# The output projection of a hybrid attention block: from eight row-and-column products to a 2x2 block product in seven multiplications

## The chip, the cores and the metric

One core of one Trainium2 chip runs the whole program. The metric is device microseconds (us) of one execution. The engines are TensorE (PE in the profile; its weight loads are PEld), VectorE (DVE), ScalarE (ACT), GpSimd (POOL) and SyncE (SP, which only issues transfers). Each engine works through its own queue in order and waits on semaphores.

## The reference, cut to what matters

A block of 512 tokens and width 1024: a gated linear attention and a latent attention run side by side, their outputs are merged by two gates, and the merged rows are projected and added to the residual. A feed-forward layer follows.

```
merged = sigmoid(z_ma) * y_gla + sigmoid(z_mb) * y_mla      # 512 x 1024
h = h + merged @ w_out                                      # 1024 x 1024 weights
m = rmsnorm(h, g_mlp)
h = h + square(relu(m @ w_ff1)) @ w_ff2
return rmsnorm(h, g_final)
```

All of it is float32. The kernel multiplies on TensorE in fp32r: each operand is split into a high and a low part (`split`, line 92: ScalarE rounds the high part, another engine subtracts it), and one product is three matmuls, high by high, high by low and low by high (`mm3`, line 87).

## The kernel before, in words

The work is laid out with features on partitions (transposed) up to the merge. `g2`, `y1` and `merged` hold one 128x512 tile for each of the eight latent heads: 128 features by 512 tokens.

**Attention** (lines 1134 to 1148). A loop over n from 0 to 37 takes one quarter of a head at each step: scores of quarter n (`att_scores`, line 903), the flip of the probabilities of quarter n-3 by TensorE transposes (`att_flip`, 921), and the values of half a head at n-6 (`att_values`, 932). Beside them `up_units` (849) projects the queries, keys and values of the next pair of heads; GpSimd subtracts the low parts of its weights. After the second half of a head VectorE multiplies the values by the gate (944) and GpSimd adds the other branch (945). A planner (the tile framework's scheduler) fixes each engine's order when the program is built, by trace order as priority and by the buffers that are free; `in_program_order` (110) overrules it for the engines that it names, from a mark on.

**Output projection** (lines 1149 to 1244). After the loop the eight merged tiles are scaled by 0.5 and split (1151). `rows_product` (1163) then makes, for each half c of the 1024 output columns, four accumulators of 128 tokens by 512 columns, each over eight feature tiles k: 2 x 4 x 8 = 64 products, 192 matmuls of 128x512. The weights come in pieces of 256 rows (`weights`, 218). For c = 1 the last two pieces are kept back so that the rows are finished one after the other: a row's sum is added to the residual `h` by VectorE (`add_rows`, 1210), squared by ScalarE (`square_half`, 171), its reciprocal root made by VectorE and GpSimd (`row_rstd`, 178), scaled by VectorE (`normed`, 1226) and turned by eight TensorE transposes (`flipped`, 1237; `Flipped.rows`, 191), and after every second row the turned tiles are read out of PSUM and split by ScalarE and VectorE (`Flipped.evacuate`, 201).

**Feed-forward** (lines 1416 to 1472). Two projections, f00 and f01, are begun early (1416, 1417 to 1424): their first half runs before the last two rows are turned. The second matrix product of each quarter already is a 2x2 block product in seven multiplications (`prep` 1275, `pair_units` 1321, `block_product` 1352): sums of blocks of the left and right side are multiplied, and the results are added to the rows.

**Buffers.** Tiles of one tag share a fixed number of buffers: 29 of 2 KB a partition (`u2`), 26 of 4 KB (`u4`), 3 staging tiles for weights (`stage`, 209), and four each for the high and the low parts of weights (`halves`, 213). A new tile waits until the last reader of the oldest buffer is done.

```
    def halves(nk, nw, name):
        wh = tl([P, nk, nw], F32R, "wh", 4, f"{name}h")
        wl = tl([P, nk, nw], F32R, "wl", 4, f"{name}l")
```

Of the kernel before, what the change touches and what calls it, by code (L numbers as in the profile page):

```python
# [18 lines left out]
P = 128  # L19
# [37 lines left out]
def tile_block(ctx: ExitStack, tc: tile.TileContext, t, out: bass.AP):  # L57
# [113 lines left out]
    def square_half(rows, c, parts, junk):  # L171
        nc.scalar.activation(
            junk[:, c * S : (c + 1) * S], rows[:, c * S : (c + 1) * S], AF.Square, accum_out=parts[:, c : c + 1]
        )
        if c == 0:
            nc.gpsimd.tensor_scalar(parts[:, 2:3], parts[:, 0:1], 1.0 / D, EPS, op0=ALU.mult, op1=ALU.add)
# [207 lines left out]
    nc.vector.tensor_scalar(gla_gain, gvec[:, V_GLA : V_GLA + 8], 0.5, None, op0=ALU.mult)  # L384
# [461 lines left out]
    merged = [None] * MH  # L846
    heads = {}

    def up_units(pr):
# [37 lines left out]
        for j in range(2):  # L887
# [7 lines left out]
            split(hl[:, 0].rearrange("p a b -> p (a b)"), hl[:, 1].rearrange("p a b -> p (a b)"), acc)  # L895
# [36 lines left out]
    def att_values(head, half):  # L932
        if half == 0:
            avs[head] = ps("mm", f"av{head}")
        acc = avs[head]
        hi, lo = pTs.pop((head, half))
        _, _, vs, c = heads[head]
        for k in range(NT):
            vt = vs[k // 2]
            mm3(acc[:, half * 256 : (half + 1) * 256], vt[:, 0, k % 2, c], vt[:, 1, k % 2, c],  # L940
                hi[:, k, :], lo[:, k, :], k == 0, k == NT - 1)
        if half == 1:
            y = g2[head]
            nc.vector.scalar_tensor_tensor(y, y, 1.0, acc, op0=ALU.add, op1=ALU.mult)  # L944
            nc.gpsimd.tensor_tensor(y, y, y1[head], op=ALU.add)  # L945
            merged[head] = y
# [186 lines left out]
    units = iter(())  # L1133
    for n in range(4 * MH + LAG_C):
# [6 lines left out]
        if 0 <= b < 4 * MH:  # L1141
            flips = traced()
            att_flip(b // 4, b % 4)
            if b == 0:
                gla_turn(GH - 1, (flips, traced()))
        c = n - LAG_C
        if c >= 0 and c % 2 == 1:
            att_values(c // 4, (c % 4) // 2)
    for i in range(MH):
        hl = u4(f"mg{i}")  # L1150
        split_scaled(hl[:, 0, :], hl[:, 1, :], merged[i], 0.5)
        merged[i] = hl


    hrow = []
    for i in range(NT):
        r = u4(f"h{i}", F32, (P, D))
        nc.scalar.dma_start(r, t["x"][0, i * P : (i + 1) * P, :])
# [4 lines left out]
    def rows_product(lhs, w, nk, name, first_done, done, flip):  # L1163
        for c in range(2):
            accs = [ps(("mm", "at")[c], f"{name}{c}{i}") for i in range(NT)]

            def piece(i, k2, wh, wl):
                tok = slice(i * P, (i + 1) * P)
                for kk in range(2):
                    k = 2 * k2 + kk  # L1170
                    mm3(accs[i], lhs[k][:, 0, tok], lhs[k][:, 1, tok], wh[:, kk, :], wl[:, kk, :],
                        k == 0, k == nk - 1)

            staggered = 2 if c == 1 else 0
            kept = []
            for k2 in range(nk // 2):
                wh, wl = weights(w[k2 * 2 * P : (k2 + 1) * 2 * P, c * S : (c + 1) * S], f"{name}{c}{k2}")
                if k2 >= nk // 2 - staggered:
                    kept.append((k2, wh, wl))
                    continue  # L1180
                for i in range(NT):
                    piece(i, k2, wh, wl)
            if c == 0:
                for i in range(NT):
                    add_rows(i, c, accs[i])
                    first_done(i)
                continue
            begun = traced()
            ks = [(2 * k2 + kk, wh[:, kk, :], wl[:, kk, :]) for k2, wh, wl in kept for kk in range(2)]

            def part(i, which):
                tok = slice(i * P, (i + 1) * P)
                for k, wh, wl in ks[which]:
                    mm3(accs[i], lhs[k][:, 0, tok], lhs[k][:, 1, tok], wh, wl, k == 0, k == nk - 1)

            def complete(i):
                add_rows(i, c, accs[i])
                done(i)

            for i in range(2):  # L1200
                part(i, slice(0, 4))
                complete(i)
            for i in range(2):
                part(2 + i, slice(0, 2 - i))
                flip(i)
                part(2 + i, slice(2 - i, 4))
                complete(2 + i)
            return begun

    def add_rows(i, c, acc):  # L1210
        hc = hrow[i][:, c * S : (c + 1) * S]
        nc.vector.tensor_tensor(hc, acc, hc, op=ALU.add)  # L1212

    fm = Flipped(gvec[:, V_MLP : V_MLP + 8], "m")
    mT = fm.out
    w1, w2 = t["w_ff1"][0], t["w_ff2"][0]
    ms_rows = {}

    def first_half_square(i):
        hparts[i] = sm(f"hp{i}", 4)  # L1220
        ms_rows[i] = u4(f"ms{i}", F32, (P, D))
        square_half(hrow[i], 0, hparts[i], ms_rows[i])
# [3 lines left out]
    def normed(i):  # L1226
        at = traced()
        m = ms_rows[i]
        square_half(hrow[i], 1, hparts[i], m)
        rs = row_rstd(hparts[i])  # L1230
        for c in range(2):
            nc.vector.tensor_scalar(
                m[:, c * S : (c + 1) * S], hrow[i][:, c * S : (c + 1) * S], rs, None, op0=ALU.mult
            )
# [9 lines left out]
    begun = rows_product(merged, t["w_out"][0], KD, "wo", first_half_square, normed, flipped)  # L1244

    NQ = 4
    FQ = DFF // P // NQ  # L1250
    NP = FQ // 2
    HT = S // 2
    B11, B12, B21, B22 = range(4)
    wq = [[u4(f"w2_{x}{g}", F32, (P, 2, S)) for g in range(NP // 2)] for x in range(4)]

    def load_w2(qd, x):
        for g in range(NP // 2):
            for pp_ in range(2):
                r = (qd * FQ + 2 * (2 * g + pp_) + x // 2) * P
                c = (x % 2) * S  # L1260
                nc.sync.dma_start(wq[x][g][:, pp_, :], w2[r : r + P, c : c + S])

    def add_w2(dst, x, y, op):
        for g in range(NP // 2):
            nc.vector.tensor_tensor(wq[dst][g], wq[x][g], wq[y][g], op=op)  # L1265

    def split_w2(x, name):
        res = []
        for g in range(NP // 2):
            wh, wl = halves(2, S, f"{name}{g}")  # L1270
            split(wh, wl, wq[x][g])
            res.append((wh, wl))
        return res

    def prep(m, qd):

        more = qd + 1 < NQ
        if m == 1:
            return split_w2(B11, f"b1_{qd}")
        if m == 2:  # L1280
            res = split_w2(B21, f"b2_{qd}")
# [3 lines left out]
        if m == 3:  # L1285
            return split_w2(B22, f"b3_{qd}")
        if m == 5:
            add_w2(B11, B12, B11, ALU.subtract)
            return split_w2(B11, f"b5_{qd}")
        if m == 6:  # L1290
            add_w2(B11, B22, B11, ALU.subtract)
            return split_w2(B11, f"b6_{qd}")
        if m == 7:
            add_w2(B12, B22, B12, ALU.subtract)
            res = split_w2(B12, f"b7_{qd}")
# [5 lines left out]
        res = split_w2(B11, f"b4_{qd}")  # L1301
# [19 lines left out]
    def pair_units(qd, p, a22):  # L1321
# [7 lines left out]
        a11, a12, a21, a22_ = px[:, 0:HT], px[:, HT:S], qx[:, 0:HT], qx[:, HT:S]  # L1329
        y, z = u2(f"y{qd}{p}"), u2(f"z{qd}{p}")  # L1330
        s1, s2, s3, s4 = y[:, 0:HT], y[:, HT:S], z[:, 0:HT], z[:, HT:S]
        g1 = u4(f"ga{qd}{p}")
        split(g1[:, 0, :], g1[:, 1, :], px)
        nc.vector.tensor_tensor(s1, a21, a22_, op=ALU.add)
# [166 lines left out]
```

## Time and profile before

| | us |
|---|---|
| median of 3 runs (769.06 to 769.26) | 769.13 |
| the profiled execution, its own time | 769.4 |
| its span, first to last instruction | 767.7 |
| PE busy in the span | 758.5 |
| DVE busy | 571.4 |
| ACT busy | 441.8 |
| POOL busy | 119.1 |

The profiled execution's time is 1.7 us above its span: what lies before the first and behind the last instruction. Shares of busy time are means over stages with different limits, so a change in one stage is read from that stage. A row of a timeline gives the start, the duration, the engine, the line, the operation, the tile written, the tiles read, the shapes and the count; in square brackets stands the engine's idle time before it and what ended it. A row's duration begins when the engine takes the instruction up, so that a wait for a shared port is part of the duration.

### The profile page before, as it was taken

The numbers are of one execution on the slowest core, as the hardware profiler recorded it, in microseconds if no ns is written. First come the engines' busy times: TensorE is split into PE (matmuls) and PEld (weight loads), VectorE is DVE, ScalarE is ACT, GpSimd is POOL, SyncE is SP. The second block draws the span as 40 slices with busy tenths as digits, with TensorE's granted clock in tenths as the row PEclk, the third lists the DMA queues.
The fourth block names the chain that finished last, engine by engine and source line by source line (L and its number), as shares of the span: only waits on it lengthen the run. The fifth ranks groups of instructions, "written<-read, shape, count | busy, mean of one in ns | idle before, by whom it ended". The sixth has DMA issues, their size and how long they took to land.

```text
span 767.7 us, 10149 instructions
## 1 busy us (share of the span) xinstructions
PE 758.5 (99%) x3768; PEld 641.4 (84%) x3768; DVE 571.4 (74%) x850; ACT 441.8 (58%) x749; POOL 119.1 (16%) x190
## 2 busy tenths in 40 slices
PE   9999999999999999999999999999999999999996
PEld 7888788889888889889988988888888888888885
DVE  7789999656767765999944776975887478848695
ACT  7556567465466555888833566434653555346644
POOL 0710005260624105111200100000000000000014
PEclk9999999999999999999999999999999999999998
DMA  9733211221334324221043721353115510550002
GB/s 314 248 111 118 81 28 28 56 77 36 85 80 108 60 53 110 73 66 55 29 165 87 270 83 56 99 181 104 55 55 175 155 30 26 188 168 1 27 1 109
DMA packets 93185, 73.94 MB, mean 96 GB/s; under 512 B 15088, under 2 KB 74480, under 8 KB 93136
## 3 DMA queue, kind: packets, MB, share of 16 engines
q1 hardware_dynamic: 92048, 70.14, 31.0%
q10 hardware_dynamic: 864, 2.38, 0.8%
q0 software_dynamic: 224, 0.79, 0.3%
q8 instruction: 29, 0.48, 0.3%
q14 instruction: 20, 0.16, 0.1%
HBM read 69.62 MB, written 2.10 MB: 93 GB/s over the span
## 4 chain that ended last, share of the span: by engine, by line
PE 96%; DVE 2%; ACT 1%; issue 0%; POOL 0%; POOLq 0%; ACTq 0%
PE f L89 8%; PE f L90 8%; PE f L88 8%; PE gx L88 4%; PE gx L89 4%; PE gx L90 4%; PE first L325 3%; PE za L88 2%; PE za L89 2%; PE wo L89 2%; PE wo L90 2%; PE gz L89 2%; PE za L90 2%; PE gz L88 2%; PE wo L88 2%; PE gz L90 2%
## 5 line engine op out<-in xcount | busy, mean ns | idle before, releaser
L1440 POOL DMA_DIRECT2D gfin<-in_g_final x1 | 0.7, 653 | 282.7 <-PE f L90 282.7
L1265 DVE TENSOR_TENSOR w<-w,w 128x1024 f32<-128x1024 f32 x32 | 38.7, 1221 | 0.4
L913 ACT ACTIVATE e<-s,top 128x512 f32<-128x512 f32 x32 | 21.8, 683 | 4.3 <-DVE top L910 4.3
L473 POOL COPY v3f<-rrf 128x4 f32<-128x4 f32 x4 | 2.8, 708 | 135.9 <-DVE rrf L456 135.9
L1212 DVE TENSOR_TENSOR h<-gx,h 128x512 f32<-128x512 f32 x32 | 21.6, 685 | 1.9 <-PE gx L90 1.8
L94 DVE TENSOR_TENSOR pT<-tp,pT 128x512 fp32r<-128x512 f32 x32 | 21.6, 679 | 0.6 <-ACT pT L93 0.4
L910 DVE TENSOR_REDUCE top<-s 128x1 f32<-128x512 f32 x32 | 21.6, 680 | 0.1
L93 ACT ACTIVATE pT<-tp 128x512 fp32r<-128x512 f32 x32 | 18.9, 592 | 3.4 <-PE tp L927 3.3
L945 POOL TENSOR_TENSOR tb<-tb,za 128x512 f32<-128x512 f32 x8 | 11.2, 1401 | 52.8 <-DVE tb L944 38.4
L927 PE MATMUL tp<-ident,e 128*128 128x128 f32 x128 | 19.2, 272 | 0.0
L88 PE MATMUL av<-pT,v 128*128 128x256 f32 x64 | 19.2, 300 | 0.0
L1318 ACT ACTIVATE fa<-f 128x512 f32<-128x512 f32 x32 | 18.5, 578 | 0.0
L89 PE MATMUL av<-pT,v 128*128 128x256 f32 x64 | 18.4, 288 | 0.0
L927 PEld LDWEIGHTS tp<-ident,e 128*128 128x128 f32 x128 | 15.5, 140 | 3.5 <-PE s L90 0.6
L90 PE MATMUL av<-pT,v 128*128 128x256 f32 x64 | 18.2, 285 | 0.0
L93 ACT ACTIVATE gbh<-y 128x512 fp32r<-128x512 f32 x16 | 10.1, 634 | 14.0 <-DVE y L1335 14.0
L94 DVE TENSOR_TENSOR sc<-sc,sc 128x512 fp32r<-128x512 f32 x16 | 10.9, 690 | 9.5 <-ACT sc L93 9.5
L93 ACT ACTIVATE sc<-sc 128x512 fp32r<-128x512 f32 x16 | 9.3, 596 | 11.5 <-DVE sc L544 11.5
L88 PE MATMUL s<-kbuf,q 96*128 96x512 f32 x32 | 13.9, 434 | 0.6 <-ACT e L913 0.3
L93 ACT ACTIVATE b_20h<-w 128x1024 fp32r<-128x1024 f32 x7 | 7.4, 1060 | 12.1 <-PE gz L90 6.0
L93 ACT ACTIVATE b_10h<-w 128x1024 fp32r<-128x1024 f32 x7 | 7.4, 1059 | 12.1 <-PE gz L90 6.0
L93 ACT ACTIVATE b_00h<-w 128x1024 fp32r<-128x1024 f32 x7 | 7.4, 1057 | 12.1 <-PE gz L90 6.0
(1569 smaller groups left out, 2889.1 us busy)
## 6 DMA issues: line engine op xcount, KB each, us to landing
w<-in_w_ff SPq DMA_DIRECT2D x64, 256.0 KB, 3.6
grw<-in_w_in SPq DMA_DIRECT2D x8, 512.0 KB, 8.6
gvw<-in_w_in SPq DMA_DIRECT2D x8, 512.0 KB, 4.7
x<-in_xt SPq DMA_DIRECT2D x8, 256.0 KB, 5.3
vw<-in_w_first SPq DMA_DIRECT2D x8, 256.0 KB, 5.4
h<-in_x ACTq DMA_DIRECT2D x4, 512.0 KB, 5.1
out<-ms SPq DMA_DIRECT2D x7, 256.0 KB, 2.2
q<-ro SPq DMA_DIRECT2D x16, 64.0 KB, 2.7
```

Of the source, the lines that this page charges most:

```text
L88: nc.tensor.matmul(acc, lh, rh, start=start, stop=False, skip_group_check=onto)
L89: nc.tensor.matmul(acc, lh, rl, start=False, stop=False, skip_group_check=onto)
L90: nc.tensor.matmul(acc, ll, rh, start=False, stop=stop, skip_group_check=onto)
L93: nc.scalar.activation(hi, src, AF.Copy)
L94: rest.tensor_tensor(lo, src, raw(hi), op=ALU.subtract)
L325: nc.tensor.matmul(f_accs[i], a[:, i * P : (i + 1) * P], b, start=k == 0 and x == 0, stop=k == KD - 1 and x == 2)
L910: nc.vector.tensor_reduce(top, acc, axis=AX.X, op=ALU.max, negate=True)
L913: nc.scalar.activation(e, acc, AF.Exp, bias=top, accum_out=tot)
L927: nc.tensor.transpose(tp[:, k * P : (k + 1) * P], e[:, k * P : (k + 1) * P], ident)
L1212: nc.vector.tensor_tensor(hc, acc, hc, op=ALU.add)
L1265: nc.vector.tensor_tensor(wq[dst][g], wq[x][g], wq[y][g], op=op)
L1318: nc.scalar.activation(a, acc, AF.Relu)
```

## The change

The output projection becomes one 2x2 block product. The left side is the merged matrix, cut by pairs of heads (an even and an odd head are the two blocks of the inner dimension) and by halves of the tokens; the right side is `w_out`, cut into blocks of 128 rows (even or odd) and 512 columns. Seven products in the order 1, 2, 5, 6, 3, 7, 4 take the place of eight; each has four pairs p, two row blocks rb and three matmuls, 24 of 128x512, and 168 in all.

- **Merge.** The factor 0.5 moves into `gla_gain` (0.25) and into the split of the values, so the merged tiles aren't scaled. GpSimd writes the sums by token halves into new tiles; the last head is merged in two halves.
- **Left sums.** At n = 13, 21 and 29 GpSimd makes the four sums of a pair (four 128x256) and the low parts of them (two 128x512); at n = 26 it makes the low parts of the first blocks of pairs 0 and 1. The sums of the last pair are VectorE's, behind the loop.
- **Right sums.** The four blocks of `w_out` are loaded by SP into the eight tiles that hold `w_ff2` later. Three sums of blocks are made by transfers that add onto a loaded tile (`load_onto`, issued by GpSimd, 2 x 512 KB each), one by VectorE.
- **Rows.** Three of the six accumulations per pair of row blocks are copied out of PSUM by ScalarE and added to `h` by GpSimd (`add_rows_by_copy`); the others are still added by VectorE. The squares of `normed` take the column halves in the order in which they come; of the two scalings in `normed` one is ScalarE's.
- **Orders.** From the end of the loop on, TensorE, ScalarE and VectorE keep program order; GpSimd keeps it from the start of the loop. The four loads of `h` go from the ACT queue to SP's. The first loads of `w_ff2` are spread among the products. f00 is begun ahead of product 7, f01 ahead of product 4.

The core of the diff:

```
+    def load_onto(dst, x, w):
+        for g, d in enumerate(block_tiles(dst)):
+            rows = w[4 * g * P : 4 * (g + 1) * P, (x % 2) * S : (x % 2 + 1) * S]
+            nc.gpsimd.dma_start(d, rows.rearrange("(k t p) w -> p t k w", t=2, p=P)[:, x // 2], accum_op=ALU.add)
...
-            split(hl[:, 0].rearrange("p a b -> p (a b)"), hl[:, 1].rearrange("p a b -> p (a b)"), acc)
+            split_scaled(*flat, acc, 0.5)
...
+        nc.vector.scalar_tensor_tensor(y[:, tok], y[:, tok], 1.0, acc[:, tok], op0=ALU.add, op1=ALU.mult)
+        for x in halves_:
+            t_ = slice(x * HT, (x + 1) * HT)
+            nc.gpsimd.tensor_tensor(merged[p][x][:, c], y[:, t_], y1[head][:, t_], op=ALU.add)
...
+        if n == 26:
+            load_w2(0, B11, w_out)
+            load_w2(0, B21, w_out)
+            for p in range(2):
+                split_first(wo_left[p], merged[p][0], f"o{p}", nc.gpsimd)
+        if n == 28:
+            wo_right[1] = split_w2(B11, "bo1")
+        if n == 29:
+            load_onto(B11, B12, w_out)
...
-    for i in range(MH):
-        hl = u4(f"mg{i}")
-        split_scaled(hl[:, 0, :], hl[:, 1, :], merged[i], 0.5)
-        merged[i] = hl
+        if c > 0 and c % 8 == 7 and c // 8 < NP - 1:
+            p = c // 8
+            y, z = merged_sums(p, nc.gpsimd)
+            split_sum(wo_left[p], y, 5, 6, f"bo{p}", nc.gpsimd)
+            split_sum(wo_left[p], z, 7, 3, f"co{p}", nc.gpsimd)
+        if n == 30:
+            load_w2(0, B12, w_out)
+            load_w2(0, B22, w_out)
+        if n == 31:
+            wo_right[2] = split_w2(B21, "bo2")
...
+    def add_rows_by_copy(i, c, acc, sign=1.0):
+        part = u2(f"part{i}{c}")
+        nc.scalar.activation(part, acc, AF.Copy, scale=sign)
+        hc = hrow[i][:, c * S : (c + 1) * S]
+        nc.gpsimd.tensor_tensor(hc, hc, part, op=ALU.add)
...
+    begun = traced()
+    xs_ = [ps("at", f"wox{rb}") for rb in range(2)]
+    zs_ = [ps("at", f"woz{rb}") for rb in range(2)]
+    ws_ = [ps("mm", f"wow{rb}") for rb in range(2)]
+    wo_accs = {2: ws_, 5: zs_, 3: zs_}
...
+    wo_product(1)
...
+    wo_right[5] = [split_part(B11, 0, "bo5")]
+    y, z = merged_sums(last, nc.vector)
+    split_sum(wo_left[last], y, 5, 6, f"bo{last}")
+    for rb in range(2):
+        add_rows_by_copy(rb, 0, xs_[rb])
+    load_onto(B12, B22, w_out)
+    wo_right[5].append(split_part(B11, 1, "bo5"))
+    wo_product(2)
+    add_w2(B11, B22, B11, ALU.add)
+    for rb in range(2):
+        add_rows(rb, 0, ws_[rb])
+        first_half_square(rb, 0)
+    wo_right[6] = split_w2(B11, "bo6")
+    load_onto(B11, B21, w_out)
+    load_w2(0, B21)
+    wo_product(5)
+    split_sum(wo_left[last], z, 7, 3, f"co{last}")
+    for rb in range(2):
+        add_rows_by_copy(2 + rb, 1, zs_[rb])
+    wo_right[3] = split_w2(B22, "bo3")
+    load_w2(0, B22)
+    for p in range(NP):
+        corner(p, nc.gpsimd if p < last else nc.vector)
+    wo_product(6)
...
+    for rb in range(2):
+        add_rows_by_copy(rb, 1, xs_[rb], -1.0)
+    wo_right[7] = split_w2(B12, "bo7")
+    load_w2(0, B12)
+    for rb in range(2):
+        wo_product(3, (rb,))
+        add_rows(rb, 1, zs_[rb])
+        normed(rb, 1)
+    wo_right[4] = split_w2(B11, "bo4")
+    load_w2(0, B11)
+    early = [proj_begin(w1, 0, "f00", "at")]
+    for rb in range(2):
+        wo_product(7, (rb,))
+        add_rows(2 + rb, 1, xs_[rb], ALU.subtract)
+        first_half_square(2 + rb, 1)
+        flipped(rb)
+    early.append(proj_begin(w1, P, "f01", "at"))
+    for rb in range(2):
+        wo_product(4, (rb,))
+        add_rows(2 + rb, 0, xs_[rb])
+        normed(2 + rb, 0)
     proj_run(early[0], mT, 0)
     proj_run(early[1], mT, 0, range(5))
     flipped(2)
...
-    in_program_order(begun, PE_ONLY)
-    for x in (B11, B12, B22, B21):
-        load_w2(0, x)
+    in_program_order(begun, PE_ONLY + SPLITTERS)
+    in_program_order(attending, (mybir.EngineType.Pool,))
```

`wo_product(m, rbs)` runs over the pairs p and, inside, over the row blocks; products 1, 6, 7 and 4 accumulate in `xs_`, product 2 in `ws_`, products 5 and 3 in `zs_`. `split_w2` and `split_part` split two, or one, of a block's 128x1024 tiles into buffers of `halves`; `split_sum` and `corner` split left sums and the last left block.

## The prediction, made before any run of the changed kernel

> **What bounds the kernel now.** I read the page first: busy time and the chain that ended last.
>
> ```profile
> PE 758.5 (99%) x3768; PEld 641.4 (84%) x3768; DVE 571.4 (74%) x850; ACT 441.8 (58%) x749; POOL 119.1 (16%) x190
> ...
> PE 96%; DVE 2%; ACT 1%; issue 0%; POOL 0%; POOLq 0%; ACTq 0%
> ```
>
> TensorE is busy nearly all the time, and 96% of the chain is its own. A matmul fewer is worth its pitch, as long as the other engines keep up. Whether they have room is seen by stage (columns: stretch, its length, then busy us and instructions of PE, PEld, DVE, ACT, POOL, granted clock, share of DMA, GB/s):
>
> ```profile
> 320.00:340.00 20.00, 20.00 (x138) 18.00 (x137) 18.92 (x39) 18.21 (x41) 2.85 (x5) 1.00 0.16 54
> ...
> 360.00:384.00 24.00, 23.73 (x172) 21.49 (x171) 22.58 (x47) 19.90 (x45) 5.50 (x4) 1.00 0.07 24
> 385.70:430.40 44.70, 44.70 (x208) 37.16 (x206) 20.10 (x30) 14.12 (x27) 4.53 (x8) 1.00 0.52 173
> ```
>
> The first two are attention: VectorE is at 94%, ScalarE at 83 to 91%. The third is the output projection: VectorE half idle, GpSimd at a tenth. The pitch of its matmuls comes from the instructions of one weight piece to the same place two pieces on:
>
> ```profile
> L88 PE MATMUL wo<-wo01h,mg x8: 389/389/389, 390.5 to 395.3; 128*128 128x512 f32 x8
> ...
> L88 PE MATMUL wo<-wo03h,mg x8: 389/389/389, 401.4 to 406.1; 128*128 128x512 f32 x8
> ```
>
> 48 matmuls take 401.4 - 390.5 = 10.9 us, so 0.227 us each. The 389 ns is the pipeline's length, not the pitch.
>
> **The change part by part. Matmuls.** 192 become 168: 24 x 0.227 = **5.4 us** less; the loops fix that count, so that part can't fail. One product (24) is 5.44 us, one row block of it 2.72.
>
> **Work that is traded evenly.** The eight scalings of merged tiles go, and the left splits come. The four 128x1024 splits of weights that attention now holds (half of `w_out`) stay four (products 1 and 2). The value split only gets a factor. The loads of `h` cross from ACT's to SP's queue, and the first loads of `w_ff2` from one block behind the projection's issues to four places among its products; their readers come behind three pairs of feed-forward projections, so I count nothing. If that cover went, a late load would cost about its landing, 3.6 us.
>
> ```profile
> w<-in_w_ff SPq DMA_DIRECT2D x64, 256.0 KB, 3.6
> ```
>
> **GpSimd against VectorE.** This decides the case. In the first stage both read SBUF:
>
> ```profile
> 35.97 1.75 DVE L94 TENSOR_TENSOR gr11l<-grw,gr11h 128x1024 fp32r<-128x1024 f32 x1
> ...
> 34.92 1.72 POOL L576 TENSOR_TENSOR xz<-x,xy 128x256 f32<-128x256 f32 x1
> 36.60 1.72 POOL L575 TENSOR_TENSOR xz<-x 128x256 f32<-128x256 f32 x1
> 38.29 0.73 POOL L576 TENSOR_TENSOR xz<-x,xy 128x256 f32<-128x256 f32 x1
> ...
> 30.54 0.68 DVE L374 SCALAR_TENSOR_TENSOR gqn<-first,R 128x512 f32<-128x512 f32 x1
> ...
> 30.61 0.73 POOL L566 TENSOR_TENSOR xy<-xy,x 128x256 f32<-128x256 f32 x1
> ```
>
> They take turns: the low part of a weight (two SBUF inputs) takes 1.75 us in place of 1.23 (row of f00l below), and a GpSimd sum 1.72 in place of 0.73, so **1.0 us** more for each that meets a low part. At 30.5 VectorE reads PSUM (`first`), and neither is longer. The Trainium skill, "SBUF — State Buffer", section "Who interferes with whom", states this as an exclusive lock between a VectorE instruction with two SBUF inputs and a GpSimd instruction that reads SBUF; the trace agrees (1.72 us against 0.73).
>
> **Attention.** GpSimd gains 3 x (4 x 0.73 + 2 x 1.38) + 2 x 1.38 = 20 us, ScalarE 8 high parts of 0.63 = 5 us. What GpSimd meets on VectorE is the scaling L916:
>
> ```profile
> L945 POOL TENSOR_TENSOR tb<-tb,za x8: 1277/1380/1674, 327.0 to 386.7; 128x512 f32<-128x512 f32 x8
> ...
> 369.78 1.28 POOL L945 TENSOR_TENSOR tb<-tb,za 128x512 f32<-128x512 f32 x1 [7.09 <-DVE tot L914]
> 370.29 1.07 DVE L916 TENSOR_SCALAR e<-e,tot 128x512 f32<-128x512 f32 x1
> ...
> 373.91 0.49 DVE L916 TENSOR_SCALAR e<-e,tot 128x512 f32<-128x512 f32 x1
> ```
>
> 0.58 us each; I take four more, 2.3 us, against 1.1 and 1.4 us of VectorE idle in the two stretches above (44 us). Flips run three quarters behind, which hides most of it. Bounds: nothing, and 3 us (all of the 2.3 and some of ScalarE's 5). I take 0.6, near the bound of nothing, because of that lag, and because PE is busy for all but 0.27 of the 24 us around the scaling that met GpSimd at 370.29.
>
> **The order behind the loop.** VectorE, ScalarE and GpSimd now go strictly in program order. Durations:
>
> ```profile
> 412.52 1.06 ACT L93 ACTIVATE f00h<-f00f 128x1024 fp32r<-128x1024 f32 x1 [3.82 <-issue]
> ...
> 413.61 1.23 DVE L94 TENSOR_TENSOR f00l<-f00f,f00h 128x1024 fp32r<-128x1024 f32 x1 [4.26 <-ACT f00h L93]
> ...
> 424.51 1.03 PE L197 MATMUL mb<-ident,ms 128*128 128x128 f32 x8
> 430.06 3.23 DVE L98 SCALAR_TENSOR_TENSOR mT<-mb,gvec,mT 128x256 fp32r<-128x256 f32 x8
> 433.20 0.69 DVE L1212 TENSOR_TENSOR h<-wo,h 128x512 f32<-128x512 f32 x1
> 433.92 0.63 ACT L172 ACTIVATE ms<-h 128x512 f32<-128x512 f32 x1 [1.69 <-DVE h L1212]
> 434.46 0.19 ACT L172 ACTIVATION_READ_ACCUMULATOR ms<-h 128x1 f32 x1
> 434.68 0.16 DVE L179 SCALAR_TENSOR_TENSOR hp<-hp 128x1 f32<-128x1 f32 x1 [0.79 <-ACT ms L172]
> 434.92 0.55 POOL L182 TENSOR_TENSOR hp<-hp,mhalf 128x1 f32<-128x1 f32 x1 [5.69 <-DVE hp L179]
> 435.50 0.88 DVE L1232 TENSOR_SCALAR ms<-h,hp 128x512 f32<-128x512 f32 x2 [0.66 <-POOL hp L182]
> ```
>
> From a row's addition to its scaled halves is 433.20 to 436.1 = **2.9 us**, the later half now ScalarE's copy (0.62). Low parts follow each other at 1.14 (1.23 less an overlap of 0.08). A flip holds PE 0.8 (424.51 to the next matmul at 425.31). I set zero where PE has only the projection left (385 us), and walk the queues:
>
> 1. *Product 6* (PE at 16.3). VectorE, behind product 1: the four sums, low parts (one waits for a row sum of GpSimd), two weight additions 2 x 1.14, two row additions 2 x 0.6, done at 14.1. ScalarE's two squares stand ahead of weight 6: high 14.9 to 16.0, low to 17.2. **PE waits 0.9.**
> 2. *Flip of row 0.* GpSimd's queue from 17.3: the adding transfers of product 4's weight (issue 0.7 each by the row of `gfin` below, the second behind the second low part of weight 6, at 18.4), done at 19.1. Then six sums, row 0's the last: 2 x 1.38, three corners 3 x 0.70, one 1.38, in all 6.2, and 3.9 of turns lost to the four low parts of weights 3 and 7: row 0's sum is done at 29.2. Product 3's row block 0 ended at 16.3 + 0.9 + 5.4 + 2.7 = 25.4. VectorE's addition to the same half row must wait for GpSimd's; 29.2 + 2.9 = 32.1. PE wants the flip behind product 7's row block 0, at 25.4 + 2.7 + 2.7 = 30.8. **PE waits 1.2.**
> 3. *Product 4.* It accumulates onto `xs_`, so it waits for `add_rows` of product 7. Queued ahead of that on VectorE: row 1's chain (to 34.1), two low parts of weight 4 and f00's low part. The high ones on ScalarE stand behind row 1's copy; lows run 35.8 to 39.2, the addition to 39.8. f00 also needs one of the four weight buffers, free only three quarters through product 7's row block 1. PE is there at 32.1 + 0.8 + 2.7 + 0.8 = 36.4. **PE waits 3.4.**
> 4. *Flip of row 3.* Behind the start of product 4 VectorE owes 1.3 of row additions, 3.2 of read-out, f01's low part 1.2 and two chains of 2.9, with the waits for ScalarE between them 11.4 us; PE has 5.4 + 39 matmuls of 256 columns at half of 0.227 (4.4) + 0.8 = 10.6. **PE waits 0.8.**
>
> ```profile
> L1440 POOL DMA_DIRECT2D gfin<-in_g_final x1 | 0.7, 653 | 282.7 <-PE f L90 282.7
> ```
>
> Sum: 0.9 + 1.2 + 3.4 + 0.8 = 6.3 back, 0.6 in attention, 5.4 gained: +1.5 us. Against the profiled execution's own time: 769.4 + 1.5 = **770.9**; the median of before lies 0.3 under it. 0.2%, about what a measurement of this kernel can tell from no change, is 1.5 us, so same is 767.6 to 770.7 and the forecast lies on its upper edge.
>
> **Rivals.**
>
> *A, the forecast* (chance 0.42): the queues lose 5 to 9 us, 769 to 773, by the ends of the turns (none to two more) and of attention.
>
> *B, GpSimd is in time* (0.40). If the turns cost little, because the low parts fall between GpSimd's sums, terms 1 and 2 go (2.1). Term 3 stays in part, by the buffer rule: behind the freed buffer come 1.06 + 1.23 + 0.69 = 3.0 us, and PE has 1.4 of product 7 and 0.8 of a flip left, 0.8 at least; with the low parts of weight 4 (2.3) behind row 1's chain at most 3.1. I take the middle, 2.0. With term 4: 769.4 - 5.4 + 2.0 + 0.8 = 766.8; range 765.5 to 769. For it: GpSimd has only some 15 us to do in these 45 (six sums of 1.38, three corners, four issues, four roots of 0.55). Against: most of it can't start before weight 6 is split.
>
> *C, attention pays* (0.10). GpSimd's bursts and ScalarE's 5 us hit a stage where three engines are over 83% busy; from 2.5 us of VectorE delay on PE waits. 3 us in place of 0.6: 773.3, to 776.
>
> *D, an adding transfer lands late* (0.08). No row shows one. Lower bound 3.6 us (256 KB, plain), upper twice the 8.6 us of a slow 512 KB load, as it reads its target too:
>
> ```profile
> grw<-in_w_in SPq DMA_DIRECT2D x8, 512.0 KB, 8.6
> ```
>
> I take 6, nearer to the plain loads. It hurts from about 12 on (weight 7 is issued at 11 behind two row sums, and wanted by ScalarE at 23). At 17 PE waits 5 more: 776. The Trainium skill, "DMA: Bandwidth & Descriptors", section "Anatomy of one DMA — SWDGE (gpsimd) path", gives about 2.0 us plus bytes over 436 GB/s, an estimate of 3.2 us for 512 KB; by that this rival falls away and the sum stays. No run here shows it for a transfer that adds.
>
> **How the numbers follow.** Faster: 0.31 of B. Same: 0.09 of B, 0.16 of A: 0.25. Slower: 0.26 of A, C and D: 0.44. Range: from the middle of B (766) to the near ends of C and D (775); A alone 769 to 773.
>
> **What would show it.** 168 matmuls on wo tiles with a pitch of 0.227. PE's idle time: a gap ahead of product 6, of the first `mb` flip, of product 4 (the largest, ended by `h`, VectorE) and of the fourth flip. Right for A: GpSimd sums at 1.7 to 2.3 us beside low parts, row 0's sum ending 3 us or more behind product 3's row block 0. Wrong: no gap ahead of the first flip (B), scores waiting in attention (C), high parts of weights 5, 7 or 4 waiting for a transfer (D).

## The result, and the profile after

| | before | after |
|---|---|---|
| median, us | 769.19 (4 runs, 769.06 to 769.30) | 790.9 (4 runs, 789.9 to 793.0) |
| ratio, 95% interval | | 1.0286 (1.0264 to 1.0308) |
| the profiled execution | 769.4 | 790.3 |

The changed kernel is 2.9% slower. The forecast was 770.9, within 766 to 775. From the page of the changed kernel, the same two rows as before and the issues of the adding transfers (count, KB, median us from issue to landing):

```profile
PE 759.9 (96%) x3744; PEld 641.1 (81%) x3744; DVE 587.2 (74%) x857; ACT 456.4 (58%) x774; POOL 157.2 (20%) x233
...
PE 84%; issue 5%; DVE 4%; POOL 3%; ACT 3%; POOLq 0%; DVEq 0%; ACTq 0%
...
w<-in_w_out POOLq DMA_DIRECT2D x6, 512.0 KB, 6.8
```

TensorE has 24 matmuls fewer, as counted, and yet no less busy time; its share of the chain falls from 96% to 84%, and the rest now lies with the three other engines and with issue (time in which an engine waits for nothing that the profile shows). Where TensorE waits, its waits from 300 to 470 us tell (who waited, for what, us in all, times, longest):

```profile
PE tp L1024 <- ACT e L1015: 5.7, 1, 5.7
PE woz L89 <- DVE bo30l L94: 5.1, 1, 5.1
PE s L88 <- ACT e L1010: 4.7, 2, 2.5
PE wox L88 <- DVE h L1289: 1.1, 1, 1.1
PE tp L1024 <- DVE pT L94: 0.9, 1, 0.9
PE tp L1024 <- ACT e L1010: 0.7, 1, 0.7
PE wox L89 <- DVE bo60l L94: 0.7, 1, 0.7
PE mb L198 <- DVE ms L1311: 0.6, 1, 0.6
PE f L89 <- DVE mT L98: 0.6, 1, 0.6
```

The rows with `tp` and `s` are attention: 5.7 + 4.7 + 0.9 + 0.7 = **12.0 us**, where the forecast had 0.6. `woz <- bo30l` is product 3, **5.1 us**, where it had nothing. The other four together are 3.0. In the kernel before, the same view of the same stretch has two rows, 0.5 us in all:

```profile
PE s L88 <- ACT e L913: 0.3, 1, 0.3
PE s L88 <- DVE pT L94: 0.2, 1, 0.2
```

**Attention.** The longest of these waits ends at an exponential (`e`; `tp` are the transposes of `e`, `pT` their copies for the values, `s` the scores). The timelines of ScalarE and GpSimd ahead of it (start, us, engine, line, tiles; in brackets the idle time before and what ended it):

```profile
389.65 0.63 ACT L93 ACTIVATE ghbo<-yo 128x512 fp32r<-128x512 f32 x1 [3.83 <-POOL yo L929]
391.02 0.63 ACT L93 ACTIVATE ghco<-zo 128x512 fp32r<-128x512 f32 x1 [0.74 <-POOL zo L931]
391.55 0.67 ACT L1010 ACTIVATE e<-s,top 128x512 f32<-128x512 f32 x1
```

```profile
386.34 1.61 POOL L928 TENSOR_TENSOR yo<-my 128x256 f32<-128x256 f32 x1
388.03 1.59 POOL L929 TENSOR_TENSOR yo<-yo,mx 128x256 f32<-128x256 f32 x1
389.58 0.72 POOL L930 TENSOR_TENSOR zo<-mx,my 128x256 f32<-128x256 f32 x1
390.26 0.72 POOL L931 TENSOR_TENSOR zo<-mx,yo 128x256 f32<-128x256 f32 x1
```

ScalarE stands idle for 3.83 us at the high part `ghbo`, which waits for GpSimd's sum `yo`, and again at `ghco` for `zo`. The high parts aren't wanted before the projection, but the planner put them in ScalarE's queue ahead of the exponential `e`, which TensorE needs at once. The same group stands at 343 us (1.60 idle) and at 367 us (1.80); those are the two waits of `s`.

**Product 3.** VectorE and GpSimd around the low part that TensorE waits for:

```profile
417.80 2.46 POOL L908 DMA_DIRECT2D w<-in_w_out  x2 [2.23 <-DVE bo60l L94]
418.56 0.68 DVE L94 TENSOR_TENSOR glco<-zo,ghco 128x512 fp32r<-128x512 f32 x1
419.65 8.73 DVE L94 TENSOR_TENSOR bo30l<-w,bo30h 128x1024 fp32r<-128x1024 f32 x1 [0.41 <-ACT bo30h L93]
419.70 3.12 POOL L1295 TENSOR_TENSOR h<-h,part 128x512 f32<-128x512 f32 x2
422.21 2.65 POOL L94 TENSOR_TENSOR gdo<-my,gdo 128x256 fp32r<-128x256 f32 x3
424.28 3.00 POOL L1295 TENSOR_TENSOR h<-h,part 128x512 f32<-128x512 f32 x2
```

`bo30l` takes 8.73 us in place of 1.23: it gets no turn until seven GpSimd instructions, which follow the issue of two adding transfers, are done at 427.28.

**The clock.** By stretch (busy us of PE, PEld, DVE, ACT, POOL, then the granted clock):

```profile
345.80:352.00 6.20, 6.20 (x37) 5.42 (x38) 4.97 (x13) 5.71 (x14) 5.99 (x8) 1.00 0.36 95
...
393.60:396.00 2.40, 2.35 (x10) 2.31 (x11) 1.98 (x4) 1.91 (x4) 1.39 (x2) 0.50 0.99 348
396.00:400.00 4.00, 4.00 (x18) 3.39 (x16) 1.23 (x3) 1.07 (x3) 0.10 (x1) 0.61 0.76 299
...
428.40:433.30 4.90, 4.86 (x12) 3.86 (x13) 3.72 (x4) 0.00 (x0) 0.00 (x0) 0.50 0.75 230
```

Behind the two waits of over 5 us TensorE runs at half clock: 2.4 x 0.50 + 4.0 x 0.39 + 4.9 x 0.50 = **5.2 us** lost, nearly all of the 5.4 us that the missing matmuls take off its busy time. Behind the 2.5 us wait at 343 the clock stayed whole. The account: 12.0 + 5.1 + 3.0 + 5.2 = 25.3, less 0.5 of waits that before had too and 5.4 of matmuls, is 19.4 of the 20.9 between the two profiled executions; the other 1.5 isn't accounted for.

### The profile page after: what moved, and what is told of

Its sections match the earlier page's. It is cut to its first block, busy times and chain, and to the rows that moved or that the text cites. A ratio compares the mean times of both kernels' runs of the same rounds, so it can differ in the third digit from the quotient of the medians.

```text
span 788.6 us, 10218 instructions
## 1 busy us (share of the span) xinstructions
PE 759.9 (96%) x3744; PEld 641.1 (81%) x3744; DVE 587.2 (74%) x857; ACT 456.4 (58%) x774; POOL 157.2 (20%) x233
## 4 chain that ended last, share of the span: by engine, by line
PE 84%; issue 5%; DVE 4%; POOL 3%; ACT 3%; POOLq 0%; DVEq 0%; ACTq 0%
PE f L89 7%; PE f L90 7%; PE f L88 7%; PE gx L88 4%; PE gx L90 4%; PE gx L89 4%; PE first L326 3%; PE za L88 2%; PE za L90 2%; PE za L89 2%; PE gz L88 2%; PE gz L90 2%; PE gz L89 2%; PE zb L88 1%; PE zb L90 1%
## 5 line engine op out<-in xcount | busy, mean ns | idle before, releaser
L912 DVE TENSOR_TENSOR w<-w,w 128x1024 f32<-128x1024 f32 x34 | 41.1, 1219 | 0.3
L1289 DVE TENSOR_TENSOR h<-h,gx 128x512 f32<-128x512 f32 x32 | 21.5, 680 | 1.9 <-PE gx L90 1.8
L88 PE MATMUL av<-pT,v 128*128 128x256 f32 x64 | 19.8, 309 | 0.0
L89 PE MATMUL av<-pT,v 128*128 128x256 f32 x64 | 19.1, 299 | 0.0
L90 PE MATMUL av<-pT,v 128*128 128x256 f32 x64 | 18.5, 290 | 0.0
L93 ACT ACTIVATE ghb<-y 128x512 fp32r<-128x512 f32 x16 | 10.1, 632 | 14.0 <-DVE y L859 14.0
L1055 POOL TENSOR_TENSOR mx<-tb,za 128x256 f32<-128x256 f32 x8 | 6.5, 816 | 50.0 <-DVE tb L1052 50.0
L173 ACT ACTIVATE ms<-h 128x512 f32<-128x512 f32 x8 | 5.0, 628 | 18.7 <-DVE h L1289 18.7
```

The costliest lines, as they stand in the source:

```text
L88: nc.tensor.matmul(acc, lh, rh, start=start, stop=False, skip_group_check=onto)
L89: nc.tensor.matmul(acc, lh, rl, start=False, stop=False, skip_group_check=onto)
L90: nc.tensor.matmul(acc, ll, rh, start=False, stop=stop, skip_group_check=onto)
L93: nc.scalar.activation(hi, src, AF.Copy)
L1289: nc.vector.tensor_tensor(hc, hc, acc, op=op)
```

## The experiments

Theory 1: a high part that waits for a GpSimd sum blocks ScalarE's queue in attention. Theory 2: a run of GpSimd instructions behind a transfer's issue shuts VectorE out in product 3. Rivals: GpSimd's load on the shared port as such, the adding transfers themselves, or engines that are simply full. Every ratio is to the kernel before, with its 95% interval.

**late_splits**

```diff
-            y, z = merged_sums(p, nc.gpsimd)
-            p = c // 8
-            y, z = merged_sums(p, nc.gpsimd)
+            sums[c // 8] = merged_sums(c // 8, nc.gpsimd)
+        if n in (16, 24, 35):
+            p = (16, 24, 35).index(n)
+            y, z = sums[p]
             split_sum(wo_left[p], y, 5, 6, f"bo{p}", nc.gpsimd)
             split_sum(wo_left[p], z, 7, 3, f"co{p}", nc.gpsimd)
```

> The sums of the heads stay GpSimd's and stay where they are; only the splits of the first three pairs of sums are issued later (three quarters of a head on for pairs 0 and 1, behind the last scores for pair 2), so that their high parts no longer stand in ScalarE's queue ahead of exponentials. Theory 1 (ScalarE's queue: a high part that waits for a GpSimd sum holds back the exponentials behind it): the gaps of TensorE in attention, 2.5, 2.7, 0.9, 1.1 and 5.9 us, fall to under 1 us together, and with the last one goes the half-speed stretch behind it, some 2.5 us; the projection keeps its 5.3 us gap in product 3. 790.9 - 15 = 776, between 774 and 779. Rival (the sums cost VectorE its turns, or ScalarE is simply overloaded): the same work in the same stage keeps the gaps, 788 to 791.

783.0 us, ratio 1.0181 (1.0164 to 1.0198): 8 us less with the same work, where 15 was expected: below the range of the rival (788 to 791), but above that of the theory (774 to 779). Its waits of TensorE, the first three:

```profile
PE woz L89 <- DVE bo30l L94: 5.1, 1, 5.1
PE tp L1024 <- DVE pT L94: 2.3, 1, 2.3
PE uq L90 <- POOL wq3l L94: 1.6, 1, 1.6
```

The waits for `e` at 343, 367 and 388 us (10.4 together) are gone, so theory 1 holds for the waits. Two new ones stand in their place. `wq3l`, the low part of a weight of the next heads, now stands in GpSimd's queue behind the two late low parts. And `pT` stands on VectorE behind a scaling of `e` that took 2.07 us beside two merges of GpSimd, right behind an adding transfer's issue.

**no_adding_transfers** and **late_splits_no_adding**: `load_onto` is replaced by `add_w2` on VectorE, three times two additions of 128x1024, without and with the late splits.

```diff
-    load_onto(B12, B22, w_out)
...
+    add_w2(B12, B12, B22, ALU.add)
+    load_w2(0, B22)
     wo_right[7] = split_w2(B12, "bo7")
```

> The three weight sums that adding transfers made are made by VectorE (two additions of 128x1024 each, 1.2 us apiece, 7 us in all), and the loads of w_ff2 into the kept blocks move behind them. Nothing else. Theory (GpSimd's queue piles up behind the issue of the adding transfers, and what follows in one piece shuts VectorE out): the 8.7 us low part of weight 3 falls to 1.2 to 3, the 5.3 us gap in product 3 goes, the third wait in attention shrinks by the 2.5 us of two issues; against that VectorE's 7 us cost 1 to 5: 783 to 788. Rival (GpSimd's sums and corners run into VectorE wherever they stand): a low part of 5 us or more stays, 790 to 796. The two earlier gaps in attention (2.5 and 2.7) stay under both.

> Both edits: the splits issued later, and VectorE makes the weight sums. If the two losses are separate the gains add: 776 less 2 to 7, so 769 to 774. If the gap in product 3 only followed from the late start of the projection, the second edit brings nothing, or its 7 us of VectorE: 776 to 780.

793.0, ratio 1.0314 (1.0297 to 1.0331), and 783.3, 1.0184 (1.0169 to 1.0199): no gain in either, and the second lies above both of its ranges (769 to 774, 776 to 780). The long low part is gone (`bo30l` took 2.32 and 2.31 us, in turns with the same GpSimd sums), but TensorE now waits 4.7 us ahead of product 4 and 0.8 to 2.5 each at weights 6 and 7: VectorE's additions are 7 us of queue. So they cost about what the transfers cost; whether it is the adding, the issue or the run behind it that hurts, this doesn't tell. In attention the first of the two shows something that theory 1 leaves out: the wait of 5.7 us is down to 1.1 (a new one, for `pT`, is 2.7), so the adding transfers issued there had a part in it.

**late_splits_rows_by_vector**

```diff
-        add_rows_by_copy(rb, 0, xs_[rb])
+        add_rows(rb, 0, xs_[rb])
...
```

> The splits issued later, and the six additions of rows that went by a copy on ScalarE and a GpSimd sum (1.4 us each) are made by VectorE straight from PSUM (0.6 us each, 3.6 in all). The adding transfers and the corners stay. Theory (a run of GpSimd instructions with SBUF inputs shuts VectorE out): with four of the seven instructions of that run gone, the low part of weight 3 takes 3 to 5 us in place of 8.7, and product 3 loses at most 1: 771 to 775. If the adding transfer itself holds the port, the 8.7 us stays: 776 to 779.

776.4, ratio 1.0094 (1.0079 to 1.0109), above the theory's 771 to 775, though its signs came. `bo30l` takes 3.15 us beside the three corners that are left of the run, and product 3 loses 0.3. Now the wait ahead of product 4 stands at its full size:

```profile
PE wox L88 <- DVE h L1292: 3.1, 1, 3.1
```

**splits_behind_weights**, **weight4_early**, **adding_behind_sums**: one move each, one upon the other (each edit against the run before it).

```diff
-        if n in (16, 24, 35):
+        if n in (19, 24, 35):
...
+        if rb == 1:
+            wo_right[4] = split_w2(B11, "bo4")
         normed(rb, 1)
-    wo_right[4] = split_w2(B11, "bo4")
-    early = [proj_begin(w1, 0, "f00", "at")]
...
-        if n == 29:
-            load_onto(B11, B12, w_out)
...
             sums[c // 8] = merged_sums(c // 8, nc.gpsimd)
...
+            load_onto(B11, B12, w_out)
```

> As late_splits_rows_by_vector, with the first pair's splits three steps later still, so that their two GpSimd low parts (2.6 us) stand behind the low parts of the last heads' up-projection weights in GpSimd's queue and not ahead of them. Theory (the 1.8 us gap at 347 us is TensorE waiting for the weights' low part, which waits in GpSimd's queue): the gap goes, 776.4 - 1.8 = 774.6, 773.5 to 775.5. Rival (GpSimd is simply full there): the gap moves and stays, 776 to 777.

> As splits_behind_weights, and the split of weight 4 stands ahead of row 1's norm, the two first weights of w_ff1 behind both row additions of product 7. Theory (the 3.3 us gap ahead of product 4 is VectorE's queue: two low parts of weight 4 and one of f00 ahead of the row addition that product 4 waits for): the gap falls to at most 0.5, and of it 0 to 1 comes back where f00 is wanted: 774.6 - 2.8 = 771.8, 771 to 773. Rival (the gap is set by when the rows are done, not by what is queued ahead): no gain, 774 to 775.

> As weight4_early, and the first adding transfers are issued behind the sums of the third pair of heads, not ahead of the merges of that pair. Theory (GpSimd's queue waits 2 us for the weight's low part before it can issue, then runs the merges in one piece and holds up VectorE's scaling of e, 2.1 us in place of 0.5): the gaps at the end of attention, 2.5 and 0.8 us, fall to 1 us together and the half-speed stretch of 2 us behind them goes: 771.8 - 3 = 769, 767.5 to 770.5. Rival (VectorE and ScalarE are full there whatever GpSimd does): 771 to 773.

774.7, 773.3 and 771.6 (1.0075, 1.0056, 1.0028; the last 1.0017 to 1.0040). The first is as expected: the wait for `wq3l` is gone. In the second the 3.1 us ahead of product 4 are gone, but only 1.4 came through to the time: 1.7 us of waits at the flips (`mb <- ms`) and 0.9 at the first feed-forward projections stand where the run before had none over 0.2. Of the third, 1.75 of 3 came through; the waits that it aimed at shrank, but 771.6 lies in the range of its rival (VectorE and ScalarE are full there). So queue order, together with the row sums that went back to VectorE, takes 790.9 to 771.6.

**sums_by_vector** (its edit against adding_behind_sums)

```diff
-            sums[c // 8] = merged_sums(c // 8, nc.gpsimd)
+            sums[c // 8] = merged_sums(c // 8, nc.vector)
```

> As adding_behind_sums, but the first three pairs of sums are VectorE's (12 of 0.42 us, 5 us, in place of 12 of 0.73 or more on GpSimd). If GpSimd is the right engine for them: VectorE, over 90% busy in that stage, passes 1 to 4 us on to TensorE, 770 to 773. If what GpSimd costs VectorE in turns is worth more than the sums: 767 to 769, no slower than adding_behind_sums.

779.2, ratio 1.0135 (1.0120 to 1.0151), slower than either range said (770 to 773, 767 to 769). VectorE's queue shows why:

```profile
341.03 1.22 DVE L928 TENSOR_TENSOR yo<-my 128x256 f32<-128x256 f32 x1 [0.94 <-POOL my L1055]
...
384.76 0.43 DVE L928 TENSOR_TENSOR yo<-my 128x256 f32<-128x256 f32 x1 [1.72 <-POOL my L1055]
```

A sum at the head of VectorE's queue waits for GpSimd's merge, and the `pT` behind it is late (waits of TensorE for `pT`: 8.1 us in all, where adding_behind_sums has 1.1). It is theory 1 on another engine; how much of the 7.6 us is VectorE's load, this run doesn't separate.

**projection_tuned** and **queue_order_last**: attempts to clear the waits that were left.

```diff
+    wo_right[2] = [split_part(B21, 0, "bo2")]
...
+        if rb == 1:
+            early = [proj_begin(w1, 0, "f00", "at")]
         first_half_square(2 + rb, 1)
```

> As adding_behind_sums, and each remaining wait of TensorE that a queue explains is moved: the split of weight 2 goes from the last scores to behind them (gaps of 1.0 and 0.8 at 380 to 383 us), the splits of pair 2 behind the first halves of the last pair (1.0 at 391), the second half of weight 4 behind row 1's norm (0.8 at 423), f00 ahead of the flips' read-out (0.4 at 431), f01 between row 2's root and its scaling (1.3 at 437). If the seven products only lose to queue order, these 5.3 us go but for 1 to 2: 771.6 - 3.8 = 767.8, 766.5 to 769.3, at or below before's 769.2 with 5.4 us fewer matmuls. Rival (VectorE and ScalarE are full from 370 to 440 us, and a wait that is moved comes back elsewhere): 770 to 772.

> As adding_behind_sums, with two moves only: the second half of weight 4's split behind row 2's addition, and f01's split between the norms of rows 2 and 3. Theory (the waits left in the projection are VectorE's order): the gaps of 0.8 us ahead of the first flip and 1.3 us ahead of row 3's go: 771.6 - 1.7 = 769.9, 769.2 to 770.8. Rival (VectorE is full there, and a wait that is moved comes back, as in projection_tuned): 771 to 773.

773.9 (1.0061, 1.0047 to 1.0075) and 773.0 (1.0048, 1.0035 to 1.0061): both behind adding_behind_sums, the first by more than even its rival's 770 to 772. The theories failed, and a wait that was moved came back, as the rivals said; that the engines are full is not shown by that. In the first the gap ahead of product 4 came back (1.9), in the second four waits for f00 and f01 (0.8 to 1.1 each) took the place of the two that went. No version here beats the kernel before.

**clock_after_idle**

```diff
+            for _ in range(AGAIN.get((qd, j), 0)):
+                nc.scalar.activation(begun_[0], raw(begun_[0]), AF.Copy)
+            acc = proj_run(begun_, mT)
```

> The kernel before, in whose feed-forward stage, at full pitch otherwise, ScalarE writes the high part of seven weights 8 to 18 times more (same values), so that TensorE stands idle for different times, up to some 15 us, with full work around each. Theory (a long idle costs a stretch at half clock as well): behind a gap of 5 us or more the 512-column pitch is 0.43 us for 2 to 6 us, then 0.227; behind a gap of under 2.5 us it stays 0.227. Rival (the slow stretches of the changed kernel belong to something else in that stage, the transfers or the many small flips): no slow pitch behind any gap here.

By stretch: full pitch, a gap of 2.56 us, and what follows; then a gap of 2.2 us and what follows; a gap of 9.7 us and what follows; and what follows a gap of 3.1 us:

```profile
461.00:463.00 2.00, 2.00 (x10) 1.65 (x10) 2.00 (x3) 2.00 (x3) 0.00 (x0) 1.00 0.00 0
463.08:465.64 2.56, 0.39 (x2) 0.00 (x0) 2.56 (x4) 2.56 (x5) 0.00 (x0) 1.00 0.00 0
465.70:467.10 1.40, 1.40 (x6) 1.18 (x7) 0.45 (x1) 1.40 (x3) 0.00 (x0) 1.00 0.00 0
467.10:470.50 3.40, 3.40 (x9) 2.60 (x8) 1.23 (x1) 0.05 (x1) 0.00 (x0) 0.51 0.67 194
...
587.00:589.20 2.20, 0.46 (x3) 0.04 (x1) 1.73 (x3) 2.17 (x6) 0.00 (x0) 1.00 0.00 0
590.00:593.40 3.40, 3.40 (x9) 2.48 (x8) 3.20 (x8) 2.21 (x3) 0.00 (x0) 0.51 0.00 0
...
631.60:641.20 9.60, 0.35 (x2) 0.00 (x0) 6.02 (x10) 9.56 (x14) 0.00 (x0) 0.65 0.33 95
641.80:644.40 2.60, 2.60 (x8) 2.00 (x6) 0.00 (x0) 0.00 (x0) 0.00 (x0) 0.50 0.00 0
...
816.60:818.00 1.40, 1.40 (x6) 1.00 (x6) 1.40 (x5) 0.46 (x2) 0.00 (x0) 1.00 0.00 0
```

The half clock belongs to the gaps, not to the stage. Where gaps of 2.2 to 4.7 us (from the start of the last matmul to the start of the next) had a drop, it came 0.6 to 1.4 us after the gap's end and lasted 3.4 to 3.5 us. In gaps of 4.8, 9.7 and 13 us it came inside the gap (the mean clock in the one of 9.7 us is 0.65), and 3.4 to 5.3 us of work followed at half clock. So a gap with a drop costs half of that, 1.7 to 2.7 us, on top of its length. The lower bound of the theory failed: it kept the full pitch under 2.5 us, and 2.2 was enough. But the length of one gap doesn't decide it. Of two gaps of 3.1 us behind the same wait, one had a drop (at 698 us, clock 0.50) and one had none (at 816); in the changed kernel's attention, gaps of 2.6 and 2.8 us had none; and in sums_by_vector two waits of 1.6 and 0.6 us in a row, up to 346 us, had one (0.50 from 347 to 350). Each gap of 4.7 us and more here had one.

**gpsimd_runs**, **gpsimd_runs_behind_issue**, **gpsimd_sums_behind_large_issue**, **large_issue_right_ahead**: GpSimd sums in the feed-forward stage of the kernel before, alone and behind issues of transfers, in one execution each (the edit of the last is shown, in part).

```diff
+        if p == 2 and qd > 0:
+            land = [u4(f"land{qd}{x}", F32) for x in range(2)]
+            hs = [u2(f"hs{qd}{x}") for x in range(3)]
...
+                    nc.gpsimd.dma_start(land[x], rows, **({"accum_op": ALU.add} if qd == 1 else {}))
+            for n in range(7):
+                nc.gpsimd.tensor_tensor(hs[n % 3], px, qx, op=ALU.add)
```

> The kernel before, with ten GpSimd sums of 128x256 added in the feed-forward stage beside VectorE's own sums, once each on its own (reading one tile, writing two halves of a scratch tile in turn), once in a chain, where each reads what the one before wrote. Nothing reads the results. Theory (independent GpSimd instructions follow each other without a gap, and a VectorE instruction with two SBUF inputs gets in only at the end of the run; in a chain it gets in at each step): beside the first run one VectorE instruction takes 5 us or more, beside the chain none takes over 1.5 and the chain's sums take some 1.1 to 1.7. Rival (they take turns in both, and the 8.7 us has to do with the adding transfers' issue): no VectorE instruction over 2 us in either.

> As gpsimd_runs, with two small transfers (128x256 each, into a scratch tile) issued by GpSimd behind the first of ten sums: adding ones ahead of independent sums in the second quarter of the feed-forward stage, adding ones ahead of a chain in the third, plain ones ahead of independent sums in the fourth. Theory (sums that are queued behind a transfer's issue start overlapping and leave VectorE no turn): beside the nine sums of the second quarter, and of the fourth if the issue and not the adding counts, one VectorE instruction with two SBUF inputs takes 4 us or more and the sums start 0.7 us or less apart; beside the chain turns are taken as before. Rival (it is something in that place of the projection: the operands, or VectorE's own order): turns of 0.96 to 1.3 us in all three, as without the issues.

> The kernel before, with eight GpSimd sums of 128x512 added in the feed-forward stage beside VectorE's own; ahead of them GpSimd issues two 512 KB transfers into scratch tiles: adding ones in the second quarter, plain ones in the third, none in the fourth. Nothing reads the results. Theory (a large transfer's issue just ahead lets the sums run without a turn for VectorE): one VectorE instruction with two SBUF inputs takes 5 us or more beside the sums of the second quarter, and of the third if the issue alone counts; in the fourth turns are taken, 1.75 for a low part. Rival (the issue has no part in it, and what decides is something of the projection): turns in all three quarters, no VectorE instruction over 2.5 us.

> As gpsimd_sums_behind_large_issue, with the scratch tiles filled by GpSimd from the pair's own values, so that the two issues of 512 KB stand right ahead of seven sums of 128x512: adding in the second quarter, plain in the third, none in the fourth. Nothing reads the results. Theory (a large transfer's issue right ahead lets the sums run without a turn for VectorE): one VectorE instruction with two SBUF inputs takes 5 us or more in the second quarter, and in the third if the issue alone counts; in the fourth turns of 1.5 to 1.8. Rival (the issue has no part in it): turns in all three, nothing over 2.5 us.

The first refutes the reading of theory 2 that a run of independent sums is enough: ten of them took turns with VectorE (its sums 0.96 us in place of 0.42) just as a chain did. The second seems to refute the issue too, with 128 KB transfers: no VectorE instruction over 1.75 us beside sums of 128x256. The third told nothing, since its issues ran 30 us ahead of the sums. The fourth has the issues right ahead (adding, plain, none; the last view ends at 750 us, with five of the seven sums):

```profile
556.29 2.55 POOL L1338 DMA_DIRECT2D land<-in_w_ff  x2
557.35 10.45 DVE L1345 TENSOR_TENSOR y<-qx 128x256 f32<-128x256 f32 x1
557.92 9.59 POOL L1340 TENSOR_TENSOR hs<-px,qx 128x512 f32<-128x512 f32 x7
...
650.57 1.52 POOL L1338 DMA_DIRECT2D land<-in_w_ff  x2
651.63 9.43 DVE L1345 TENSOR_TENSOR y<-qx 128x256 f32<-128x256 f32 x1
652.09 8.68 POOL L1340 TENSOR_TENSOR hs<-px,qx 128x512 f32<-128x512 f32 x7
...
742.93 1.51 DVE L1345 TENSOR_TENSOR y<-qx 128x256 f32<-128x256 f32 x1
744.11 7.97 POOL L1340 TENSOR_TENSOR hs<-px,qx 128x512 f32<-128x512 f32 x5
```

The same VectorE sum takes 10.45 us behind two adding issues of 512 KB, 9.43 behind two plain ones, and 1.51 without. It starts while the second issue runs, and waits for all seven sums. So it is the issue, adding or not, seen once each way; why 128 KB didn't do it stays open (there too VectorE sums started during the second issue, and took 0.96 to 1.14 us).

**issue_behind_corners**: the same in place, from late_splits.

```diff
-    load_onto(B11, B21, w_out)
...
     for p in range(NP):
         corner(p, nc.gpsimd if p < last else nc.vector)
+    load_onto(B11, B21, w_out)
```

> As late_splits, with one thing moved: the adding transfer for weight 4 (and the load behind it) is issued behind the three corners, not ahead of two row sums and the corners; all GpSimd sums stay. Theory (the issue ahead of the run shuts VectorE out): the low part of weight 3 takes at most 2.5 us in place of 8.7, the gap of 5.3 us and the half-speed stretch behind it go, 783 - 6 = 777, 775 to 779. Rival (the seven GpSimd instructions do it wherever the issue stands): the 8.7 us and the gap stay, 782 to 784.

780.9, ratio 1.0149 (1.0133 to 1.0164); 777 was expected, 775 to 779. `bo30l` is down to 2.32 us beside the row sums and the corners, as the theory said; the victim is now what runs beside the issue in its new place:

```profile
411.86 2.32 DVE L94 TENSOR_TENSOR bo30l<-w,bo30h 128x1024 fp32r<-128x1024 f32 x1
413.06 4.27 POOL L94 TENSOR_TENSOR gdo<-my,gdo 128x256 fp32r<-128x256 f32 x3
...
417.28 2.45 POOL L908 DMA_DIRECT2D w<-in_w_out  x2
418.34 5.04 DVE L94 TENSOR_TENSOR bo71l<-w,bo71h 128x1024 fp32r<-128x1024 f32 x1
```

TensorE waits 1.7 us for `bo71l` in place of 5.1 for `bo30l`, and 3.4 ahead of product 4 in place of 1.1.

## Why the prediction was wrong

- **Matmuls**, 5.4 us less: right, 168 on `wo` tiles. The half clock hid it in the busy time.
- **Attention**, "I take 0.6", bounds 0 and 3: this step failed, 12.0 us of waits and 2.8 of half clock behind the last. It counted GpSimd's 20 us as turns lost by VectorE and ScalarE's 5 us as load. It didn't ask what the eight high parts wait for and what is queued behind them, and the three quarters of lag on which it leaned gave no cover, since the exponentials stood behind the high parts. The walk through the queues that I made for the projection was needed here first: late_splits took 8 us out without taking an instruction away. Rival C named the stage and the sign (scores waiting in attention), with half clock and queue left out, and its 3 us were a fifth.
- **Turns**, step 2: failed in direction. It had GpSimd lose 3.9 us to VectorE's low parts; behind the issues, VectorE's low part of weight 3 lost 7.5 us to GpSimd (8.73 less 1.23). So TensorE, not GpSimd, was late, by 5.1 us in product 3, and no wait of 1.2 stood ahead of row 0's flip (by the step's own figures, 32.1 less 30.8, it is 1.3). That turns alternate is right where no large issue runs, and the rows that I argued from had none.
- **Product 6**, 0.9: 0.7. **Flip of row 3**, 0.8: 0.6.
- **Product 4**, 3.4: 1.1 in the changed kernel, since TensorE was already late from product 3; 3.1 (late_splits_rows_by_vector) and 3.4 (issue_behind_corners) where that gap was 0.3 and gone. The queue named was the right one: weight4_early took the wait away.
- **Rival D**: a transfer landed after 6.8 us (I took 6), and no wait of TensorE names one. The estimate of 3.2 us from the Trainium skill, "DMA: Bandwidth & Descriptors", section "Anatomy of one DMA — SWDGE (gpsimd) path", was half of that for a transfer that adds; nothing hung on it.
- **The clock** had no term: 5.2 us, a quarter of the loss.

With the queue in attention, the run behind the issue and the wait of product 4 mended as far as I could, the seven products end at 1.0028 of before. The 24 matmuls are gone there, but TensorE's busy time is only 2.9 us lower (755.6 against 758.5), and its waits from 300 to 470 us are 5.9 us against 0.5. Waits that were moved late on came back in part. That VectorE and ScalarE have no room for the added work is my reading and not shown: from 370 to 440 us they are busy for 81% and 64% (62% and 48% in the kernel before), and an order without these waits isn't ruled out.

## What to carry to other kernels

When work for a later stage is given to an idle engine, look at who consumes it: the consumer's instruction stands in an in-order queue and blocks what is urgent behind it until the idle engine is done. Issue it only when its input is surely there. And keep GpSimd's own instructions, and VectorE's urgent ones, away from the issue of large GpSimd transfers.

## What the runs showed of the hardware

A VectorE instruction with two SBUF inputs that began during GpSimd's issue of 512 KB transfers waited for every GpSimd instruction queued behind (seven, 9.4 to 10.5 us; 8.73 us in the changed kernel), while without the issue they alternated (1.5 us). The Trainium skill, "SBUF — State Buffer", section "Who interferes with whom", calls the ports that the two share an exclusive lock, which whoever issues first holds for the whole instruction; the runs agree without an issue (1.51 against 0.41 us), and behind one the block lasts through seven instructions.

A gap of TensorE could cost more than its length: behind 2.56 us, and behind 2.2 us, the granted clock was 0.51 for 3.4 us, while behind one of 3.1 us it stayed 1.00. The Trainium skill, "TensorE: Matmul & The Clock Gate", section "Part 1: The HAM clock gate", puts the drop behind an idle window of about 3.4 us and the return behind 3.4 us of work; the return agrees (3.4 us, though up to 5.3 us behind gaps of 4.8), while gaps shorter than that window were enough here.
